# Hybrid decoder layer on one core: prompt attention without GpSimd, joined scores, longer decode waits

## The chip, the cores and the metric

One core of a Trainium2 chip runs the whole program. The metric is device microseconds from the start to the end of one execution; the median of several executions counts. The kernel before takes 2168.27 us (median of three, 2166.78 to 2168.47).

## The reference

One layer of a decoder runs for a prompt of 512 tokens and, with the same weights, for 8 sequences that each add one token to a cached window of 2048. All is in float32.

```
h = rmsnorm(x);  q, k, v, vc, gate_b, gate_c = split(h @ w_in)      # 2048 -> 6 x 1024
q, k = rmsnorm per head (16 heads of 64)
o = softmax over three dilated windows (128 step 1, 512 step 4, 2048 step 16) with a bias per distance
y = gate_b * conv3(gate_c * vc)
x += concat(rmsnorm(o), rmsnorm(y)) @ w_out
x += square(relu(rmsnorm(x) @ w_up)) @ w_down                       # 2048 -> 8192 -> 2048
```

The results are x, the new keys, values and convolution rows, and the cached windows moved on by one token.

## The kernel before

The 520 tokens (512 of the prompt, 8 of decode) are the columns of every matmul, in two halves of 260, and features lie on the partitions. A float32 operand is held as a rounded high part and the rest as a low part, and a product is three matmuls (high by high, high by low, low by high). ScalarE makes the high part by a copy into the rounded type, VectorE the low part by a subtract: lines 148 and 149 for the weights of the first stages, 419 and 420 for queries and keys, 482 and 483 for probabilities.

The program has a foreground and a background. The foreground is a row of projections. Each has 128 output features: two halves of the contraction, each of 8 blocks of 6 matmuls (`block`, line 213 holds the matmul). The first 24 projections are query, key and value for 8 pairs of heads; the next 24 are the three inputs of the convolution, 8 times; then come the output projection and the two layers of the MLP, which take the time after about 675 us.

The background is written as generators. `block` calls `step` twice per block, after its third and after its sixth matmul. A step moves on the first generator in `bgn` (norms of queries and keys) and then the first in `bg` (attention). A `yield` gives the turn back, and `wait(n)` yields n times, so a wait is a number of steps and thereby a place in the instruction order. All engines take their instructions in the order in which the program issues them: nothing is moved afterwards. After the fourth block of each half of a projection the weights of a later half are split (lines 148, 149). `drain` runs the steps that are left without any foreground between them; it is called after the 24 projections of the convolution (line 734).

After a query or key projection `ev_qkv` copies the result out of its bank with the norm's factor (line 529), squares it (lines 534 to 537, the squares again as a high and a low part), and puts `norm_gen` into `bgn`, to start 24 steps later, and not before the scores of the pair before are done. `norm_gen` sums the squares per head on TensorE (line 408, twice, once per half of the tokens), finishes the norm on ScalarE (411, 412) and VectorE (414 to 417), and writes the high and low parts of the normed rows (419, 420). After the value projection `attn_gen` is put into `bg`. It works on one pair of heads:

- transposes of the 8 decode rows and of the values (lines 433 to 444);
- for each of four query tiles of 128 rows: scores of both heads (`products`, line 456, into two banks from `stile`), bias, maximum and exponential (`score`, 463 to 466), division by the sum (`norm_p`, 472 and 473), and transposes of the first head's probabilities (`trans`, line 479 on TensorE into a bank from `wtile`, emptied by 482 and 483);
- the first head's product with the values (`pv`, line 489, emptied by 494 and 495);
- the second head's four transposes and its product.

The banks of PSUM: `mm` has two pairs for projections; `wtile` has two banks, which norms, transposes and the decode attention take in turn; `stile` has two, for scores and the products with the values. The third use of a name waits until the first has been read.

`dec_gen` follows the eighth pair in `bg` and runs beside the projections of the convolution: scores of the 8 decode tokens against gathered keys (VectorE, lines 603 and 609), softmax (629 to 636), transposes of the probabilities (641), then for each token three groups of gathered values: multiply (664), add (669), and a sum over the partitions on TensorE (674). At its end the sums are copied (680), transposed (684) and copied into the attention's result (687).

Of the kernel before, what the change touches and what calls it, by code (L numbers as in the profile page):

```python
# [25 lines left out]
F32 = mybir.dt.float32  # L26
# [11 lines left out]
E = 64  # L38
# [46 lines left out]
def hymba_kernel(ctx, tc, xT, wi, wo, wu, wd, state_k, state_v, sconv, relb, relrep, ohp, lcp, ohd, lcd,  # L85
# [118 lines left out]
    def wtile():  # L204
        return p2.tile([128, 512], F32, name="pw", bufs=2)
# [219 lines left out]
    def attn_gen(j):  # L425
        while done.get(("norm", j)) != 2:
            yield
        if j not in TB:
            load_T(j)
        yield from wait(1 if j else 10)  # L430
        st = wtile()
        for i in range(3):
            T.transpose(st[:NB, i * 128:(i + 1) * 128], flat(RAW[i, j])[:, SEQ:], ident)
        yield from wait(3)
        stg = wt((NB, 3, 128), name="stg")
        S.activation(stg.rearrange("p a b -> p (a b)"), st[:NB, :384], AF.Copy)
        SP.dma_start(scr_qkv[:, :, j * 128:(j + 1) * 128], stg)
        st = wtile()
        for s in range(4):
            T.transpose(st[:, s * 128:(s + 1) * 128], flat(RAW[2, j])[:, s * 128:(s + 1) * 128], ident)  # L440
        yield from wait(3)
        sv = st.rearrange("p (s h e) -> p h s e", s=4, h=2)
        S.activation(vv[:, :, :, 0], sv, AF.Copy)
        V.tensor_tensor(vv[:, :, :, 1], sv, vv[:, :, :, 0].bitcast(F32), OP.subtract)
        yield
        pt = {}

        def products(tb):

            w = (tb + 1) * 128  # L450
            q = slice(tb * 128, (tb + 1) * 128)
            ss = [stile() for _ in range(2)]
            for n, (a, b) in enumerate(((qh, kh), (qh, kl), (ql, kh))):
                for hp in range(2):
                    r = slice(hp * E, (hp + 1) * E)
                    T.matmul(ss[hp][:, :w], a[r, q], b[r, :w], start=n == 0, stop=n == 2)
            return ss

        def score(hp, tb, s):
            w = (tb + 1) * 128  # L460
            lg = late(j, tb) if hp else wt((128, 512), name="lg")
            sm = wk.tile([128, 4], F32, name="sm", bufs=8)
            V.tensor_tensor_reduce(out=lg[:, :w], in0=s[:, :w], in1=TB[j][:, hp, 512 - w:], scale=1.0, scalar=-3e38,
                                   op0=OP.add, op1=OP.max, accum_out=sm[:, 0:1])
            V.tensor_scalar(sm[:, 1:2], sm[:, 0:1], -1.0, None, op0=OP.mult)
            S.activation(lg[:, :w], lg[:, :w], AF.Exp, bias=sm[:, 1:2], accum_out=sm[:, 2:3])
            pt[hp, tb] = lg, sm

        def norm_p(hp, tb):
            w = (tb + 1) * 128  # L470
            lg, sm = pt[hp, tb]
            V.reciprocal(sm[:, 3:4], sm[:, 2:3])
            V.tensor_scalar(lg[:, :w], lg[:, :w], sm[:, 3:4], None, op0=OP.mult)

        def trans(hp, tb):
            lg, sm = pt.pop((hp, tb))
            st = wtile()
            for s in range(tb + 1):
                T.transpose(st[:, s * 128:(s + 1) * 128], lg[:, s * 128:(s + 1) * 128], ident)
            sv = st.rearrange("p (s t) -> p s t", s=4)[:, :tb + 1]  # L480
            q = slice(tb * 128, (tb + 1) * 128)
            S.activation(pth[:, :tb + 1, q], sv, AF.Copy)
            V.tensor_tensor(ptl[:, :tb + 1, q], sv, pth[:, :tb + 1, q].bitcast(F32), OP.subtract)

        def pv(hp):
            st = stile()
            for s in range(4):
                for n, b in enumerate((pth, ptl)):
                    T.matmul(st[:, s * 128:], vv[:, hp, s].rearrange("p c e -> p (c e)"), b[:, s, s * 128:],
                             start=s == 0 and n == 0, stop=s == 3 and n == 1, skip_group_check=True)  # L490
                yield
            r = slice(hp * E, (hp + 1) * E)
            o = flat(R3[:, j])[r, :SEQ]
            S.activation(o, st[:E, :], AF.Copy)
            V.tensor_tensor(o, st[E:, :], o, OP.add)
            yield

        for tb in range(4):
            ss = products(tb)
            for hp in range(2):  # L500
                score(hp, tb, ss[hp])
            yield from wait(4)
            if tb == 3:
                done["scores"] = j + 1
            for hp in range(2):
                norm_p(hp, tb)
            yield from wait(4)
            if tb:
                trans(0, tb - 1)
            yield from wait(3)  # L510
        if j < 6:
            toeplitz(j + 2)
        trans(0, 3)
        yield from wait(5)
        yield from pv(0)
        for tb in range(4):
            trans(1, tb)
            yield from wait(4)
        yield from wait(2)
        yield from pv(1)  # L520

    def ev_qkv(t, j, ps):
        raw = wt(name="raw")
        RAW[t, j] = raw
        if isinstance(ps, tuple):
            for h in range(2):
                V.tensor_tensor(raw[:, h], ps[h][:, :HT], rstd[:, h], OP.mult)
        else:
            V.tensor_tensor(raw, ps[:, :, :HT], rstd, OP.mult)
        if t == 1 and j:  # L530
            load_T(j)
        if t < 2:
            sh, sl_ = (wk.tile([128, 2, HT], F32R, name="sq", tag=g_, bufs=n_) for g_, n_ in (("w", 16), ("g", 4)))
            S.activation(sh, raw, AF.Square)
            sq = wt(name="tmp")
            P.tensor_tensor(sq, raw, raw, OP.mult)
            P.tensor_tensor(sl_, sq, sh.bitcast(F32), OP.subtract)
            hi, lo = (qh, ql) if t == 0 else (kh, kl)
            bgn.append([24 if j else 30, j, norm_gen(j, raw, (sh, sl_), qkgt[:, t:t + 1], hi, lo, okT[:, j] if t else None)])
        else:  # L540
            SP.dma_start(ovT[:, j], flat(raw)[:, :SEQ])
            bg.append(attn_gen(j))
# [18 lines left out]
    def dec_gen():  # L561
# [72 lines left out]
        yield from wait(2)  # L634
        V.reciprocal(sm[:, 3:4], sm[:, 2:3])
        V.tensor_scalar(lg, lg, sm[:, 3:4], None, op0=OP.mult)
        yield from wait(2)
        yield from wait(2)
        st = wtile()
        for g in range(3):  # L640
            T.transpose(st[:NP[g], g * 128:(g + 1) * 128], lg[:, GOFF[g]:GOFF[g] + NP[g]], ident)
# [17 lines left out]
        for n in range(len(items) + 1):  # L659
# [6 lines left out]
            if n and items[n - 1][1]:  # L666
# [2 lines left out]
                V.tensor_tensor(a[:NP[g]], a[:NP[g]], tiles.pop(("v", b, g))[:NP[g]], OP.add)  # L669
                if g == 2:  # L670
                    a = tiles.pop(("v", b, 0)).rearrange("p h e -> p (h e)")
                    yield from wait(10)
                    for c in range(4):
                        T.matmul(od[32 * c:32 * c + 32, :256], sel[:, 31 - b:63 - b], a[:, 256 * c:256 * c + 256],
                                 start=b == 0, stop=b == NB - 1, skip_group_check=True)
                    prev(n + 2)
# [584 lines left out]
```

## Time and profile before

| | us |
|---|---|
| three executions | 2166.78, 2168.27, 2168.47 |
| the profiled execution, its own time | 2167.66 |
| its span, first to last instruction | 2166.0 |
| TensorE matmuls busy | 2134.5 |
| VectorE, ScalarE, GpSimd busy | 1766.3, 957.9, 68.5 |

The profile shows one execution. A stage's limit is read from the engine that has no idle time in it, and the table of waits names for each idle time the instruction whose end let the engine go on. Times inside the trace count from the span's start. The projections of query, key and value run up to about 387 us, those of the convolution up to about 675 us.

### The profile page before, as it was taken

How to read it: one execution, taken by the hardware profiler on the slowest of the kernel's cores; microseconds unless marked ns; L12 is line 12 of the kernel's file. 1: busy time of each engine (PE TensorE's matmuls, PEld its weight loads, DVE VectorE, ACT ScalarE, POOL GpSimd, SP SyncE). 2: the span in 40 equal slices, each digit the busy share in tenths (PEclk: the TensorE clock that was granted, in tenths of full speed). 3: DMA queues.
4: the chain of work that ended last, by engine and by line, in shares of the span. 5: the costliest groups of instructions: out<-in, count | busy, mean ns of one | idle time of the engine just before them, and what ended most of it. 6: DMA issues, size and time to landing. Idle time of an engine off the chain costs nothing.

```text
span 2166.0 us, 42326 instructions
## 1 busy us (share of the span) xinstructions
PE 2134.5 (99%) x17594; PEld 2105.7 (97%) x17594; DVE 1766.3 (82%) x2421; ACT 957.9 (44%) x1379; POOL 68.5 (3%) x83
## 2 busy tenths in 40 slices
PE   8999999999999999999999999999999999999999
PEld 8888999999999999999999999999999999999999
DVE  7777776698786657798888888888999999999997
ACT  5444444321223235554444444445444444444443
POOL 1001010000000000000000000002000000000000
PEclk9999999999999999999999999999999999999999
DMA  5344543476464647666776676677876666666653
GB/s 208 124 165 148 169 161 113 139 229 210 153 186 155 245 155 243 226 221 241 253 236 219 245 246 215 246 253 269 314 291 250 225 226 251 231 224 246 239 200 122
DMA packets 137935, 459.83 MB, mean 212 GB/s; under 512 B 19504, under 2 KB 49840, under 8 KB 131344
## 3 DMA queue, kind: packets, MB, share of 16 engines
q1 hardware_dynamic: 136320, 454.81, 60.4%
q0 software_dynamic: 864, 2.10, 0.5%
q8 instruction: 138, 2.26, 0.4%
q14 instruction: 53, 0.43, 0.1%
q10 hardware_dynamic: 560, 0.22, 0.0%
HBM read 414.31 MB, written 181.16 MB: 275 GB/s over the span
## 4 chain that ended last, share of the span: by engine, by line
PE 63%; DVE 4%; ACT 1%; issue 1%; DMA 1%; DVEq 0%; SPq 0%
PE mn L1030 29%; PE mm L1030 29%; PE mm L213 5%; DVE R L788 1%; DVE wlo L149 1%; DVE wlo L788 1%; DVE x1t L934 0%; DVE acc L927 0%; DMA ra<-scr_a 0%; ACT sq L925 0%; ACT whi L148 0%; ACT x L936 0%; ACT R L936 0%; ACT R L787 0%; DMA ovs<-state_v 0%
## 5 line engine op out<-in xcount | busy, mean ns | idle before, releaser
L213 PE MATMUL mm<-R,whi 128*128 128x260 f32 x4000 | 677.7, 287 | 5.7 <-ACT whi L148 5.6
L213 PEld LDWEIGHTS mm<-R,whi 128*128 128x128 f32 x4000 | 560.8, 189 | 19.0 <-issue 8.6
L1030 PE MATMUL mm<-R,whi 128*128 128x260 f32 x3008 | 547.7, 283 | 1.7 <-ACT cs L1113 1.2
L1030 PE MATMUL mn<-R,whi 128*128 128x260 f32 x3008 | 547.5, 283 | 0.0
L1030 PEld LDWEIGHTS mm<-R,whi 128*128 128x128 f32 x3008 | 463.3, 188 | 2.1 <-ACT cs L1113 1.4
L1030 PEld LDWEIGHTS mn<-R,whi 128*128 128x128 f32 x3008 | 463.3, 188 | 0.1
L1030 PE MATMUL mn<-R,wlo 128*128 128x260 f32 x1504 | 425.0, 283 | 2.4 <-DVE wlo L788 2.4
L1030 PE MATMUL mm<-R,wlo 128*128 128x260 f32 x1504 | 425.1, 283 | 1.3 <-DVE wlo L788 1.3
L213 PE MATMUL mm<-R,wlo 128*128 128x260 f32 x2000 | 404.0, 284 | 0.0
L788 DVE TENSOR_TENSOR wlo<-raw,whi 128x1024 fp32r<-128x1024 f32 x255 | 311.9, 1223 | 109.3 <-ACT whi L787 107.5
L787 ACT ACTIVATE whi<-raw 128x1024 fp32r<-128x1024 f32 x255 | 269.3, 1056 | 207.4 <-PE mn L1030 95.3
L213 PEld LDWEIGHTS mm<-R,wlo 128*128 128x128 f32 x2000 | 310.0, 189 | 0.4
L787 ACT ACTIVATE whi<-rg 128x1024 fp32r<-128x1024 f32 x186 | 197.3, 1061 | 215.9 <-PE mn L1030 91.5
L1030 PEld LDWEIGHTS mn<-R,wlo 128*128 128x128 f32 x1504 | 283.2, 188 | 3.0 <-DVE wlo L788 3.0
L1030 PEld LDWEIGHTS mm<-R,wlo 128*128 128x128 f32 x1504 | 283.2, 188 | 1.8 <-DVE wlo L788 1.7
L788 DVE TENSOR_TENSOR wlo<-rg,whi 128x1024 fp32r<-128x1024 f32 x186 | 228.1, 1226 | 1.5 <-ACT whi L787 1.4
L148 ACT ACTIVATE whi<-raw 128x1024 fp32r<-128x1024 f32 (+1 forms) x129 | 133.7, 1038 | 167.5 <-PE mm L213 134.0
L149 DVE TENSOR_TENSOR wlo<-raw,whi 128x1024 fp32r<-128x1024 f32 (+1 forms) x129 | 155.5, 1206 | 45.6 <-ACT whi L148 43.6
L848 DVE TENSOR_TENSOR raw<-raw 128x1024 f32<-128x1024 f32 x62 | 75.6, 1219 | 0.0
L848 DVE TENSOR_TENSOR rg<-rg,raw 128x1024 f32<-128x1024 f32 x62 | 75.5, 1218 | 0.0
L848 DVE TENSOR_TENSOR raw<-rg,raw 128x1024 f32<-128x1024 f32 x60 | 73.5, 1225 | 2.1
L1150 DVE TENSOR_TENSOR yacc<-mm,yacc 128x520 f32<-128x520 f32 x96 | 66.6, 694 | 7.3 <-PE mm L1030 6.3
(227 smaller groups left out, 2291.2 us busy)
## 6 DMA issues: line engine op xcount, KB each, us to landing
oks<-state_k SPq DMA_DIRECT2D x184, 356.0 KB
ovs<-state_v SPq DMA_DIRECT2D x184, 356.0 KB
raw<-wi SPq DMA_DIRECT2D x94, 512.0 KB
raw<-wu SPq DMA_DIRECT2D x64, 512.0 KB
rg<-wd SPq DMA_DIRECT2D x64, 512.0 KB
raw<-wd SPq DMA_DIRECT2D x64, 512.0 KB
rg<-wu SPq DMA_DIRECT2D x60, 512.0 KB
raw<-wo SPq DMA_DIRECT2D x32, 512.0 KB
```

The lines of the kernel that those rows point to most:

```text
L148: S.activation(his[i][:, h], raws[i][:, h], AF.Copy)
L149: V.tensor_tensor(los[i][:, h], raws[i][:, h], his[i][:, h].bitcast(F32), OP.subtract)
L213: T.matmul(ps[t][:, :HT] if isinstance(ps, tuple) else ps[:, t, :HT], a[:, k, :], b[:, t, :], start=start and n == 0, stop=stop and n == 2)
L787: S.activation(hi, src, AF.Copy)
L788: eng.tensor_tensor(lo, src, hi.bitcast(F32), OP.subtract)
L848: e.tensor_tensor(o_, a_, b_, op)
L1030: T.matmul(ps[:, r, :HT], a[:, k, :], b(kt), start=n % 7 in ((0, 1, 3) if kts == 8 else (0, 1)) and kt == 0 and m == 0, stop=kt == kts - 1 ...
L1150: V.tensor_tensor(dst[:, r], v[:, r], dst[:, r], OP.add)
```

## The change

Four things change, all in the two attention generators and in `ev_qkv`.

- The squares of queries and keys: ScalarE squares, ScalarE copies that into the rounded type, and VectorE subtracts. GpSimd's multiply and subtract are gone.
- `products` takes a list of query tiles. Tiles 0 and 1 are computed in one go, side by side in the same two banks; tiles 2 and 3 stay single. The waits around them are now 5 steps, and the first head's transposes of tiles 0 and 1 follow the softmax of tile 2.
- The second head's transposes of tiles 0 and 2 take their bank from `stile`, those of tiles 1 and 3 from `wtile`.
- In `dec_gen` the wait ahead of the transposes of the probabilities is 10 steps instead of 4, and the wait ahead of each sum over the partitions is 14 instead of 10.

```diff
-        def products(tb):
+        def products(tbs):
             ss = [stile() for _ in range(2)]
-            for n, (a, b) in enumerate(((qh, kh), (qh, kl), (ql, kh))):
-                for hp in range(2):
-                    r = slice(hp * E, (hp + 1) * E)
-                    T.matmul(ss[hp][:, :w], a[r, q], b[r, :w], start=n == 0, stop=n == 2)
-            return ss
+            out, c = {}, 0
+            for tb in tbs:
+                w = (tb + 1) * 128
+                q = slice(tb * 128, (tb + 1) * 128)
+                for n, (a, b) in enumerate(((qh, kh), (qh, kl), (ql, kh))):
+                    for hp in range(2):
+                        r = slice(hp * E, (hp + 1) * E)
+                        T.matmul(ss[hp][:, c:c + w], a[r, q], b[r, :w], start=n == 0, stop=n == 2,
+                                 skip_group_check=True)
+                        out[hp, tb] = ss[hp][:, c:c + w]
+                c += w
+            return out
...
-        def trans(hp, tb):
+        def trans(hp, tb, st=None):
             lg, sm = pt.pop((hp, tb))
-            st = wtile()
+            st = st or wtile()
...
-        for tb in range(4):
-            ss = products(tb)
-            for hp in range(2):
-                score(hp, tb, ss[hp])
-            yield from wait(4)
-            if tb == 3:
+        ready = ()
+        for tbs in ((0, 1), (2,), (3,)):
+            both = [(hp, tb) for tb in tbs for hp in range(2)]
+            ss = products(tbs)
+            for b in both:
+                score(*b, ss[b])
+            yield from wait(5)
+            if tbs == (3,):
                 done["scores"] = j + 1
-            for hp in range(2):
-                norm_p(hp, tb)
-            yield from wait(4)
-            if tb:
-                trans(0, tb - 1)
-            yield from wait(3)
+            for b in both:
+                norm_p(*b)
+            yield from wait(5)
+            for tb in ready:
+                trans(0, tb)
+                yield from wait(3)
+            ready = tbs
+            yield from wait(1)
...
         for tb in range(4):
-            trans(1, tb)
+            trans(1, tb, None if tb % 2 else stile())
             yield from wait(4)
...
-            S.activation(sh, raw, AF.Square)
             sq = wt(name="tmp")
-            P.tensor_tensor(sq, raw, raw, OP.mult)
-            P.tensor_tensor(sl_, sq, sh.bitcast(F32), OP.subtract)
+            S.activation(sq, raw, AF.Square)
+            S.activation(sh, sq, AF.Copy)
+            V.tensor_tensor(sl_, sq, sh.bitcast(F32), OP.subtract)
...
-        yield from wait(2)
-        yield from wait(2)
+        yield from wait(10)
         st = wtile()
...
-                    yield from wait(10)
+                    yield from wait(14)
                     for c in range(4):
```

## Rows read from the trace of the kernel before

**Rows 1.** The page's first part: busy time, share of the span, instructions.

```profile
PE 2134.5 (99%) x17594; PEld 2105.7 (97%) x17594; DVE 1766.3 (82%) x2421; ACT 957.9 (44%) x1379; POOL 68.5 (3%) x83
```

**Rows 2.** TensorE's waits: waiting line, releaser, total us, times, longest.

```profile
PE pw L479 <- DVE R L483: 9.1, 11, 1.3
...
PE pw L408 <- DVE h L414: 1.5, 3, 0.9
...
PE pw L641 <- DVE lg L636: 0.9, 1, 0.9
```

**Rows 3.** Busy time by window (us; instructions), granted clock, DMA share, GB/s.

```profile
48.00:424.00 376.00, 363.80 (x2924) 345.25 (x2923) 264.15 (x633) 172.97 (x366) 33.95 (x33) 1.00 0.44 147
...
680.00:860.00 180.00, 180.00 (x1496) 179.82 (x1495) 118.87 (x184) 70.41 (x111) 1.91 (x2) 1.00 0.59 205
```

**Rows 4.** The same view, around 133 us.

```profile
131.00:132.50 1.50, 0.35 (x2) 0.14 (x2) 1.47 (x5) 0.00 (x0) 0.00 (x0) 1.00 0.12 52
...
133.20:135.60 2.40, 2.40 (x13) 2.40 (x13) 1.58 (x4) 1.39 (x3) 0.00 (x0) 0.50 0.00 0
```

**Rows 5.** Timeline, GpSimd and VectorE near 128 us, VectorE at 266: start, us, instruction.

```profile
127.66 1.06 POOL L536 TENSOR_TENSOR tmp<-raw 128x520 f32<-128x520 f32 x1 [13.15 <-DVE sm L472]
...
127.69 1.31 DVE L473 TENSOR_SCALAR lg<-lg,sm 128x512 f32<-128x512 f32 x1
...
265.96 0.49 DVE L473 TENSOR_SCALAR lg<-lg,sm 128x512 f32<-128x512 f32 x1
```

**Rows 6.** Groups by line, 48 to 424 us: count, busy us, mean ns, idle before.

```profile
L420 DVE TENSOR_TENSOR R<-raw,R 128x520 fp32r<-128x520 f32 x16 | 11.2, 697 | 6.6 <-ACT R L419 6.6
...
L534 ACT ACTIVATE sq<-raw 128x520 fp32r<-128x520 f32 x14 | 8.9, 639 | 24.5 <-DVE raw L529 24.5
```

**Rows 7.** Timeline of a steady pair, 269 to 282 us.

```profile
269.94 0.48 DVE L415 SCALAR_TENSOR_TENSOR raw<-raw,qkgt,h 128x260 f32<-128x260 f32 x1
...
271.69 0.70 DVE L529 TENSOR_TENSOR raw<-mm,rstd 128x520 f32<-128x520 f32 x1 [0.46 <-PE mm L213]
...
273.60 1.31 POOL L537 TENSOR_TENSOR sq<-tmp,sq 128x520 fp32r<-128x520 f32 x1
...
273.97 0.43 DVE L414 SCALAR_TENSOR_TENSOR h<-pw,h 128x260 f32<-128x260 f32 x1 [1.58 <-ACT h L412]
274.32 0.88 DVE L415 SCALAR_TENSOR_TENSOR raw<-raw,qkgt,h 128x260 f32<-128x260 f32 x1
...
277.10 0.55 PE L479 MATMUL pw<-ident,R 128*128 128x128 f32 x3 [0.69 <-DVE R L483]
...
277.92 1.23 DVE L149 TENSOR_TENSOR wlo<-raw,whi 128x1024 fp32r<-128x1024 f32 x1
...
280.18 0.69 DVE L483 TENSOR_TENSOR R<-pw,R 128x512 fp32r<-128x512 f32 x1 [0.56 <-ACT R L482]
...
281.50 0.63 PE L489 MATMUL pS<-R 128*128 128x512 f32 x2
```

**Rows 8.** Timeline, scores of query tiles 0 and 1 of one pair.

```profile
109.77 0.55 PE L456 MATMUL pS<-R 64*128 64x128 f32 x6
...
114.39 0.62 PE L456 MATMUL pS<-R 64*128 64x256 f32 x6
```

**Rows 9.** Timeline, end of the convolution's projections.

```profile
664.99 1.21 DVE L669 TENSOR_TENSOR kv<-kv 96x1024 f32<-96x1024 f32 x1
...
666.26 0.64 PE L674 MATMUL pw<-kv,sel 128*32 128x256 f32 x8 [1.01 <-DVE kv L669]
666.97 0.38 ACT L680 ACTIVATE os<-pw 128x256 f32<-128x256 f32 x1 [4.83 <-PE pw L674]
...
669.46 0.38 PE L684 MATMUL pw<-ident,os 128*128 128x128 f32 x2
...
674.91 0.70 DVE L719 TENSOR_TENSOR c<-mm,rstd 128x520 f32<-128x520 f32 x1 [2.55 <-PE mm L213]
...
677.83 0.69 DVE L728 TENSOR_TENSOR acc_c<-acc_c,sq 128x520 f32<-128x520 f32 x1
```

More of the change, by code (lines that the diff above doesn't have):

```diff
@@ L446, in attn_gen @@
         pt = {}
-        def products(tb):
-            w = (tb + 1) * 128
-            q = slice(tb * 128, (tb + 1) * 128)
+        def products(tbs):
             ss = [stile() for _ in range(2)]
-            for n, (a, b) in enumerate(((qh, kh), (qh, kl), (ql, kh))):
-                for hp in range(2):
-                    r = slice(hp * E, (hp + 1) * E)
-                    T.matmul(ss[hp][:, :w], a[r, q], b[r, :w], start=n == 0, stop=n == 2)
-            return ss
+            out, c = {}, 0
[10 more added lines that the diff above has]
+            return out
         def score(hp, tb, s):
```

## The prediction

> **What bounds the kernel now.** I read the page first: TensorE is busy in 99% of the span, VectorE in 82%, GpSimd in 3% [rows 1]. So time is won or lost only where TensorE waits. The table of TensorE's waits says for whom: 9.1 us at line 479, the transposes of the probabilities, until VectorE has emptied an earlier transpose bank (line 483), 1.5 us at line 408, and 0.9 us in the decode attention at line 641 [rows 2]. The windows say where: between 48 and 424 us TensorE is busy for 363.8 of 376 us and VectorE for 264, 70%; after 680 us TensorE has no gap [rows 3]. What moves the end of the two attention stages therefore moves the end of the kernel by as much. A wait also costs clock: after an idle stretch that ended at 132.5 us, in which TensorE was busy for 0.35 of 1.5 us, the granted clock was 0.50, which is 1.2 GHz [rows 4]. At half speed these 2.4 us lose 1.2, and with the flanks of the stretch I take 1.7 us for one such drop.
>
> **The unit of the sum.** In the gapless stretch 1496 matmuls take 180 us, 0.120 us each [rows 3]. The kernel calls its background generators once per three projection matmuls, so a step is 0.36 us. A projection has 32 steps, a pair of heads 96. The issue order of both kernels can be counted in steps by hand from the waits in the code.
>
> **Part 1, GpSimd's two operations become a square and a copy on ScalarE and a subtract on VectorE (16 times, two per pair).** It removes GpSimd's 1.1 and 1.3 us [rows 5, 7]; no TensorE wait names them. It returns time to VectorE: beside GpSimd line 473 took 1.31 us, by itself 0.49 [rows 5], and line 415 took 0.88 and 0.48 [rows 7]. In the steady pairs (the fourth to seventh) one of each is stretched, about 1.1 us a pair; in the first three two of line 473, 1.7 us. Over eight pairs that is about 10 us. It adds on VectorE 16 subtracts, each like line 420 (0.70 us [rows 6]), 11 us, and a wait: the subtract stands in VectorE's queue right behind line 529, which makes its input, and needs a square and then a copy of 0.64 us each on ScalarE [rows 6]. VectorE stands still for 1.4 us, 22 us over the stage. That wait is the new thing: everything behind it on VectorE is late by 2.1 us, less what was returned.
>
> Who waits for that? In a steady pair take the end of the key projection as zero, 271.4 us in the trace (line 529 follows at 271.69 [rows 7]). Now: line 414 at 274.0, the last line 483 from 280.18 to 280.87, and the second head's products with the values (line 489) at 281.50, after one wait of 0.7 to 0.9 us at the transposes at 277.10 [rows 7]. With the change VectorE's queue is, in order: line 495 (now two steps earlier, ahead of 529) to 1.15; 529 to 1.8; wait for square and copy to 3.2; subtract to 3.9; the first small 483 to 4.1; 414 to 417 to 5.8, with their ScalarE part done by 4.2; 420 behind its ScalarE copy to 7.2; the second 483 to 7.6; line 149, 1.2 us [rows 7], to 9.0; the last two 483 (0.55 and 0.69) to 10.1. TensorE reaches the products 19 steps after zero, 6.9 us, plus 0.8 us for the ten transposes on the way (three in a row last 0.55 [rows 7], so one more costs TensorE less than 0.11) and some 0.2 us around them: 7.9. So it waits **2.2 us** there. Where line 483 can start earlier than I chain it, the wait falls to nothing; where ScalarE is late as well it grows to 3. I take 2.2, since nearly every link has its duration in a row.
>
> **Part 2, half of the second head's transposes use the score banks.** The wait at 277.10 goes: the bank that those transposes now take was freed by line 495. That is -0.9 us in each of four steady pairs. But what is late next is the product above, so the four pairs together go by 4 x (2.2 - 0.9) = **+5.2**. In the first three pairs the order differs, since the first starts late; of the 10.6 us at lines 479 and 408 [rows 2] some 7 to 8 lie there, and the clock's 1.7. Walking the new order there in the same way I find 2.7 us at lines 408 and 479 and 2.0 at 489 in the first, 3.7 in all in the second (line 408 wants a bank that the new square and copy release late), 0.9 in the third: 9.3 against about 9.3. I take **0** for the three, with 5 either way; the eighth pair has no norms beside it and stays.
>
> **Part 3, the scores of the first two query tiles in one go.** Alone, six matmuls of 128 columns delay the projection matmuls by about 0.57 us, those of 256 columns by 0.64 (their rows last 0.55 and 0.62 [rows 8]), and the first projection matmul after each is followed 0.1 us late. I take 0.11 us for each of three further pairs inside a run, so the joined run costs some 0.97: 0.35 us won per pair, **-2.8** in all; between none and 0.57 x 8 = 4.6. The DMA of the bias tile moves two steps earlier on SP's queue, ahead of nothing that TensorE waits for.
>
> **Part 4, the decode attention waits longer.** Its order now: last add (line 669) 664.99, product 666.26 after 1.0 us of wait, copy 666.97, transposes 669.46 [rows 9]; the last projection matmul is issued at 674.6, 0.3 us ahead of line 719 [rows 9], 14 steps behind the transposes and 12 behind the copies that follow two steps later. The change adds 6 steps ahead of line 641 (its 0.9 us wait goes, taken as **-1**), 4 steps at each of 8 products, and takes 2 off the last prompt pair: 36. So the decode chain ends 24 steps behind the projections. The code then runs the rest at once, with no projection matmul between. Counted back from the end, the last add is 23 steps away, so add, product, copy and transposes all fall there. TensorE's queue holds the product ahead of the output projection. VectorE: lines 719 to 728 end at 678.5 as now [rows 9]; the add takes 1.2 us to 679.7. TensorE stands from 674.7: **5.0 us**. Then 0.7 to the copy, 0.4 for it and 0.2 to the transposes: 6.3 less the 0.8 us of work and the 1.0 us of wait that are there now: **+4.5**. A longer idle stretch than that of [rows 4] should cost the same clock drop: **+1.7**. If VectorE's add got in front of the convolution's work, it would be 2 us less. The kernel's two small output DMAs wait on ScalarE's queue behind the copies; nothing needs them. Value loads come up to four steps later, and stay two items ahead.
>
> **Sum**: +5.2 + 0 - 2.8 - 1 + 4.5 + 1.7 = +7.6 on the profiled execution's 2167.66, which is 0.6 below the median of 2168.27: **2175.3 us**. A measurement of this kernel can tell about 0.2% (4.3 us) from no change.
>
> **Rivals.**
> *The freed port wins (faster).* If VectorE catches up, the products with the values never wait, and the old waits (10.6 and 1.7) go with the 2.8 of part 3 and 1 of line 641; at the end the decode tail takes 6.2. That gives 2167.7 - 16.1 + 6.2 = 2158; with half of the old waits left, 2164. For it: the waits near 131 us lie right behind line 473 stretched to 1.31 [rows 5]. It decides where VectorE's new standing still falls into the 30% in which it idles anyway [rows 3]. Against: VectorE gets about 10 us and pays 33. A rule speaks for more. The Trainium skill (SBUF — State Buffer, "SBUF: two separate sides") says that VectorE and GpSimd share a port pair under an exclusive lock held for a whole instruction, the loser blocked; by it all of GpSimd's 33.9 us of the stage could come back, as much as is paid, and this rival's 2158 would be the forecast. The trace agrees for lines 473 and 415, but where 414 ran as GpSimd did, it kept its 0.43 us [rows 7], so I stay with the 10 us. Chance 0.17.
> *The new wait only replaces the old (same).* If the products wait 0.9 instead of 2.2, the four pairs give 0: 2170. For it: the chain has ten handovers, each of which I may have too slow, and TensorE's own lateness shortens the next wait. Chance 0.25; within it, that the tail of part 4 stays hidden, 2169.
> *Slower than forecast.* Each 2.2 us wait could bring a clock drop; four of them at 1.7 give 2182. The trace shows a drop after the idle stretch of [rows 4] and none after the wait at 277.10. This lies inside my forecast's chance.
>
> **How the numbers follow.** Forecast (part 1's wait and part 4's tail both there): 0.58, 2172 to 2183. Same: 0.25. Faster: 0.17. Cut at 0.2%, the first gives slower 0.58, and of the third 0.01 falls to the second: same 0.26, faster 0.16. The range takes in the same case and the mild end of the faster one: 2163 to 2183.
>
> **What would show it.** Right: TensorE waiting at line 489 for line 483 about 2 us in each of four pairs; none at 479 there; an idle stretch of about 5 us where the convolution's projections end, and the clock at half behind it; no GpSimd beside line 473. Wrong: the decode's transposes still ahead of the last projection, or line 489 never waiting, which would say that VectorE's order has slack that I did not see.

## The result, and the profile after

The changed kernel takes 2184.18 us (median of four, 2182.19 to 2184.97); the kernel before took 2167.88 in the same comparison. The ratio is 1.0076 with a 95% interval of 1.0064 to 1.0089: 16.3 us more. The sum of the prediction had 7.6 us more. The sign was right, and the time lies 1.2 us beyond the upper end of the range.

In the code after, lines from 456 on have moved: 473 is now 478, 479 is 484, 482 and 483 are 487 and 488, 489 is 494, 494 and 495 are 499 and 500, 529 is 538, the new square, copy and subtract are 544 to 546, 674 is 682, 680 is 688, 684 is 692, 719 and 728 are 727 and 736. Lines up to 420 have kept their numbers.

The page's first part, after [rows 1]:

```profile
PE 2139.8 (98%) x17594; PEld 2111.7 (97%) x17594; DVE 1762.7 (81%) x2437; ACT 968.7 (44%) x1395; POOL 27.8 (1%) x51
```

The table of waits, after [rows 2]: waiting line, releaser, total us, times, longest.

```profile
PE pw L408 <- DVE h L414: 7.4, 2, 4.2
...
PE pw L682 <- DVE kv L677: 4.8, 1, 4.8
...
PE pS L494 <- DVE R L488: 4.6, 5, 1.0
...
PE pS L494 <- ACT R L487: 2.2, 4, 0.6
...
PE pw L484 <- DVE R L488: 0.4, 1, 0.4
...
DVE sq L546 <- ACT sq L545: 22.0, 16, 1.4
```

The 9.1 us at the transposes (line 479 before, 484 now) are down to 0.4, and the wait at the old line 641 is gone. In their place stand 7.4 us at the norm's sums, 6.8 at the products with the values (4.6 for VectorE, 2.2 for ScalarE) and 4.8 in the decode attention. VectorE's new standing ahead of the subtract is 22.0 us in 16 times, 1.4 us each, the figure that the prediction chained from two ScalarE operations.

The windows, after [rows 3, 4]: us, then busy time and instructions of TensorE, its weight loads, VectorE, ScalarE and GpSimd, granted clock, DMA share, GB/s.

```profile
48.00:424.00 376.00, 358.08 (x2850) 341.35 (x2849) 254.53 (x641) 179.23 (x377) 0.78 (x5) 0.98 0.42 141
...
680.00:860.00 180.00, 174.67 (x1433) 173.34 (x1432) 112.23 (x172) 67.84 (x106) 1.92 (x2) 0.98 0.55 193
...
91.20:94.50 3.30, 3.30 (x17) 3.30 (x16) 2.12 (x5) 1.39 (x3) 0.00 (x0) 0.50 0.03 11
...
135.50:142.20 6.70, 6.04 (x28) 6.04 (x29) 4.37 (x12) 2.86 (x6) 0.00 (x0) 0.50 0.13 51
...
333.50:336.80 3.30, 3.30 (x16) 3.30 (x16) 0.00 (x0) 0.43 (x1) 0.00 (x0) 0.50 0.00 0
381.30:384.60 3.30, 3.30 (x17) 3.30 (x15) 0.00 (x0) 0.09 (x1) 0.00 (x0) 0.50 0.00 0
...
685.10:691.80 6.70, 4.87 (x26) 3.99 (x27) 1.30 (x3) 1.73 (x4) 0.00 (x0) 0.50 0.06 13
```

Read the instruction counts first. From 48 to 424 us TensorE got through 74 matmuls fewer than before, from 680 to 860 us 63 fewer; at 0.120 us each [rows 3] that is 8.9 and 7.6 us. Between the two windows it got through 14 more (2135 for 2121), since the end of the decode attention has moved beyond 680; that takes 1.7 us off, and 14.8 of the 16.3 us are found. Then the clock. Two windows of the kernel before had 1.00 [rows 3] and have 0.98 now, because in five places TensorE ran at 1.2 GHz: 20.8 us of busy time in all (3.30 + 6.04 + 3.30 + 3.30 + 4.87). Half of that, **10.4 us**, is lost. The kernel before had one such place. [rows 4] show 2.4 us of it; all of it is 3.30 us, of which half, 1.65 us, is lost:

```profile
132.60:135.90 3.30, 3.30 (x16) 3.30 (x17) 2.48 (x5) 1.39 (x3) 0.00 (x0) 0.50 0.00 0
```

These counts are those of one profiled execution. The mean clock of the changed kernel's four executions goes from 0.993 to 0.995, so the low places need not be the same in each.

The timeline of a steady pair, after [rows 7]: start, us, instruction, in brackets the idle time before it. The key projection ends at 275.9.

```profile
276.36 0.69 DVE L500 TENSOR_TENSOR R<-pS,R 64x512 f32<-64x512 f32 x1 [0.86 <-ACT R L499]
277.08 0.70 DVE L538 TENSOR_TENSOR raw<-mm,rstd 128x520 f32<-128x520 f32 x1
...
279.16 0.70 DVE L546 TENSOR_TENSOR sq<-tmp,sq 128x520 fp32r<-128x520 f32 x1 [1.38 <-ACT sq L545]
...
281.34 0.43 DVE L417 SCALAR_TENSOR_TENSOR raw<-h,raw 128x260 f32<-128x260 f32 x1
...
282.48 0.70 DVE L420 TENSOR_TENSOR R<-raw,R 128x520 fp32r<-128x520 f32 x1 [0.71 <-ACT R L419]
...
283.70 1.22 DVE L149 TENSOR_TENSOR wlo<-raw,whi 128x1024 fp32r<-128x1024 f32 x1 [0.18 <-ACT whi L148]
284.59 0.49 PE L494 MATMUL pS<-R 128*128 128x512 f32 x1 [0.57 <-ACT R L487]
...
285.31 0.68 DVE L488 TENSOR_TENSOR R<-pw,R 128x512 fp32r<-128x512 f32 x1
...
286.04 0.50 PE L494 MATMUL pS<-R 128*128 128x512 f32 x1 [0.96 <-DVE R L488]
```

Counted from 275.9, the ends of VectorE's seven lines are 1.15, 1.9, 4.0, 5.9, 7.3, 9.0 and 10.1; the prediction had 1.15, 1.8, 3.9, 5.8, 7.2, 9.0 and 10.1. TensorE stands twice, ahead of the first matmul of the product and of the second. The last projection matmuls before it, three, start at 283.49 and are issued by 283.85 (0.12 us each); the first of the product starts 0.74 us later, and the second 1.45 us after that, where two that don't wait follow each other in 0.13 (a row of this is shown further down). That is 0.74 + 1.32 = 2.1 us against the forecast of 2.2, and TensorE arrived 7.95 us after the key projection, for 7.9.

The end of the convolution's projections, after [rows 9]:

```profile
685.16 1.22 DVE L677 TENSOR_TENSOR kv<-kv 96x1024 f32<-96x1024 f32 x1
686.43 1.08 PE L682 MATMUL pw<-kv,sel 128*32 128x256 f32 x8 [4.82 <-DVE kv L677]
687.58 0.38 ACT L688 ACTIVATE os<-pw 128x256 f32<-128x256 f32 x1 [3.21 <-PE pw L682]
688.01 0.69 PE L692 MATMUL pw<-ident,os 128*128 128x128 f32 x2 [0.50 <-ACT os L688]
```

TensorE stands for 4.82 us (forecast 5.0) behind VectorE's convolution work and its last add. The same product that took 0.64 us before [rows 9] takes 1.08, and the clock of the 6.7 us that contain it is 0.50.

### The profile page after: what moved, and what is told of

It is laid out like the page before. It is cut to its first block, busy times and chain, and to the rows that moved or that the text cites. A ratio compares the mean times of both kernels' runs of the same rounds, so it can differ in the third digit from the quotient of the medians.

```text
span 2181.9 us, 42282 instructions
## 1 busy us (share of the span) xinstructions
PE 2139.8 (98%) x17594; PEld 2111.7 (97%) x17594; DVE 1762.7 (81%) x2437; ACT 968.7 (44%) x1395; POOL 27.8 (1%) x51
## 4 chain that ended last, share of the span: by engine, by line
PE 83%; DVE 9%; ACT 4%; DMA 3%; issue 1%; SPq 0%; DVEq 0%; ACTq 0%
PE mn L1038 29%; PE mm L1038 28%; PE mm L213 22%; DVE wlo L149 2%; DMA raw<-wi 1%; ACT whi L148 1%; PE pS L494 1%; PE pS L458 1%; DMA ra<-scr_a 1%; DVE R L796 1%; DVE wlo L796 1%; DVE sc L618 1%; PE pw L484 0%; DVE kv L612 0%; DVE x1t L942 0%
```

## The experiments

The waits were foreseen nearly to the tenth, yet the loss is twice the forecast. Two questions follow. **What do the parts cost one by one**, and is the wait at the products really the squares' work, as the prediction has it? The theory at this point: the square and copy hold up VectorE's queue, and the waits cost further time by the clock; the rival: the new order of the steps alone brings TensorE to the products too early. All times below are medians with the kernel before measured beside them; the interval of each ratio reaches some 2 to 4 us to either side, so a smaller difference between two kernels rests on its trace. Nothing of the computation is left out in any of these kernels; three of them add matmuls whose results are not used.

### Part 4 undone, alone, and kept busy

First the changed kernel with the decode waits of before:

```diff
-        yield from wait(10)
+        yield from wait(2)
+        yield from wait(2)
...
-                    yield from wait(14)
+                    yield from wait(10)
```

> The changed kernel with the decode waits of before (4 steps ahead of the transposes of the probabilities, 10 ahead of each sum). Theory: the decode chain ends ahead of the last projection again, so the 5.1 us of idle TensorE at the end of the convolution's projections, the 1.1 us behind it and the 6.8 us at half clock go, and the two old waits of about 1 us come back: 7 us less than the changed kernel's 2184.2, about 2177. Rival (the tail is hidden, all the loss is in the prompt attention): 2184, within 2 us.

Measured: 2177.46 against 2166.87, ratio 1.0049 (1.0034 to 1.0064): 10.6 us of the 16.3 are left, so part 4 costs 5.7. The reverse edit in the kernel before:

> The kernel before, with only the longer waits of the decode attention (10 steps and 14 steps). By the count of steps 26 are left at the end of the convolution's projections. Theory: an idle stretch of about 5 us there and half clock behind it, the two old waits gone: 6 to 7 us slower, 2174. Rival (the tail costs only where the attention ahead of it has changed): 2168.

2173.49 against 2167.35, ratio 1.0029 (1.0018 to 1.0041): 6.1 us. Its table of waits shows the standing (line 673 here is 674 of before), and line 479 as before [rows 2]:

```profile
PE pw L479 <- DVE R L483: 9.1, 11, 1.3
...
PE pw L673 <- DVE kv L668: 4.8, 1, 4.8
```

How much of that is the clock? In the changed kernel 36 matmuls of 260 columns, into a bank of `stile` that nothing reads, were put ahead of the last product:

```diff
+                    if b == NB - 1:
+                        dum = stile()
+                        for _ in range(36):
+                            T.matmul(dum[:, :HT], R0[:, 0, 0, 0, :128], R0[:, 0, 0, 0, :], start=True, stop=True)
```

> The changed kernel, with 36 projection-sized matmuls into a free score bank issued just ahead of the last sum over the partitions, so that TensorE works through most of its 5.1 us of idle time there; their results are not used. Theory (the idle stretch costs time twice, as a wait and by the clock after it): the 6.8 us at half clock behind the stretch go, 3 us less, 2181. Rival (the clock costs nothing here): 2184 or more.

2181.10 against 2167.12, ratio 1.0060 (1.0045 to 1.0075): 14.0 us in place of 16.3. The timeline and the window of that place:

```profile
681.26 4.44 PE L684 MATMUL pS<-R 128*128 128x260 f32 x36
...
686.25 0.64 PE L686 MATMUL pw<-kv,sel 128*32 128x256 f32 x8 [0.55 <-DVE kv L677]
```

```profile
685.10:691.80 6.70, 5.64 (x51) 4.95 (x50) 2.33 (x2) 1.73 (x4) 0.00 (x0) 1.00 0.05 11
```

The wait is as long as before, only filled with work, and the product is back at 0.64 us and the clock at 1.00. So the 4.82 us of standing do bring the low clock, and it costs here 2.4 us by half of the 4.87 us of busy time, on top of the standing itself; the medians say 2.3, which by themselves would be within the noise.

### Part 1 alone, and GpSimd back

In the kernel before only the squares were changed:

```diff
-            S.activation(sh, raw, AF.Square)
...
-            P.tensor_tensor(sq, raw, raw, OP.mult)
-            P.tensor_tensor(sl_, sq, sh.bitcast(F32), OP.subtract)
+            S.activation(sq, raw, AF.Square)
+            S.activation(sh, sq, AF.Copy)
+            V.tensor_tensor(sl_, sq, sh.bitcast(F32), OP.subtract)
```

> The kernel before, with only the squares of queries and keys moved from GpSimd to ScalarE and VectorE. Theory: VectorE's new wait makes the transposes at line 479 wait longer in the steady pairs than the 0.9 us of before: 4 to 12 us slower, 2172 to 2180. Rival (the end of GpSimd's hold on VectorE is worth more): 2168 or less.

2175.19 against 2166.87, ratio 1.0039 (1.0024 to 1.0054): 8.3 us slower. So the time that VectorE gets back from GpSimd does not pay for the new standing. The first of its rows of waits stands against 9.1 in 11 times [rows 2], the second is new:

```profile
PE pw L479 <- DVE R L483: 12.6, 15, 1.5
...
PE pw L479 <- DVE h L414: 1.4, 4, 0.3
```

With lines 408 and 433 these waits are 17.9 us, 11.5 before: 6.4 of the 8.3. The clock has no part in it, its mean in the profiled execution is 1.000.

The reverse edit, GpSimd's two operations put back into the changed kernel:

> The changed kernel with the squares of queries and keys as before: one square on ScalarE, multiply and subtract on GpSimd. Theory (VectorE's wait behind line 529 makes the loss): TensorE's wait at the second head's products falls from 2.1 us to under 0.7 in the fourth to seventh pair, the waits of 3.4 and 4.3 us at the norms' matmul in the first two pairs fall to 1.5 or less, and the attention's low-clock stretches (17 us) mostly go: about 2166. Rival (the joined scores and the score banks make the new waits): no stretch of these goes, 2180 or more.

2175.38 against 2166.87, ratio 1.0039 (1.0024 to 1.0054). It gave back 7.8 us, as much as the part costs alone, but 8.5 us are still lost, where full repair of the attention stage was expected. The product's wait is not gone:

```profile
PE pw L408 <- DVE h L414: 5.9, 2, 3.5
...
PE pS L494 <- DVE R L488: 4.7, 5, 1.0
...
PE pS L494 <- ACT R L487: 1.2, 4, 0.7
```

Its larger part, ahead of the second matmul, is as long as in the changed kernel; the smaller one shrinks, and the clock is 1.00 in all four steady pairs. The timeline of one of them:

```profile
234.91 0.49 PE L494 MATMUL pS<-R 128*128 128x512 f32 x1 [0.16 <-ACT R L487]
236.37 0.50 PE L494 MATMUL pS<-R 128*128 128x512 f32 x1 [0.96 <-DVE R L488]
```

So the theory falls in one point: the wait stands mostly on the new order of the steps, and the squares lengthen it by some 0.5 us. The rows say by how much that order brings TensorE forward: before, it issued the products 10.1 us after the key projection, of which some 0.8 was waiting at the transposes [rows 7]; now it reaches them after 7.95, 1.3 us earlier.

### Which queue passes the delay on

If it is VectorE's standing of 1.4 us, then the subtract can be issued nine steps later, when its input has long been there:

```diff
-            V.tensor_tensor(sl_, sq, sh.bitcast(F32), OP.subtract)
+            later.append([8, partial(V.tensor_tensor, sl_, sq, sh.bitcast(F32), OP.subtract)])
```

(`step` counts the entries of `later` down and calls each when it is due.)

> The changed kernel, with the subtract of the squares issued 9 steps later than the copy it waits for, so that VectorE finds its input ready. The same work on every engine. Theory (the wait is the cause): nearly the same gain as with GpSimd back, 2165 to 2172, and VectorE's idle time ahead of the subtract gone. Rival (the added work on ScalarE and VectorE is the cause): over 2179.

2185.72 against 2166.87, ratio 1.0085 (1.0068 to 1.0102): no gain. The timeline of VectorE in a steady pair (line 493 is 488 of the changed kernel):

```profile
281.98 0.29 DVE L493 TENSOR_TENSOR R<-pS,R 128x128 fp32r<-128x128 f32 x1 [1.54 <-ACT R L492]
...
287.50 0.69 DVE L188 TENSOR_TENSOR sq<-tmp,sq 128x520 fp32r<-128x520 f32 x1
...
288.58 0.68 DVE L493 TENSOR_TENSOR R<-pw,R 128x512 fp32r<-128x512 f32 x1
```

VectorE no longer waits for the copy of the squares, but stands for 1.54 us for the high parts of a transpose instead: ScalarE has the square and the copy, 1.3 us, in its own queue ahead of them. And the subtract, moved, now lies ahead of the last subtracts that the product wants: the idle time ahead of the product's second matmul is 1.57 us here, 0.96 in the changed kernel. The test of this reading moves ScalarE's copy as well, together with the subtract and by 19 steps, for the keys alone:

```diff
-            S.activation(sh, sq, AF.Copy)
-            V.tensor_tensor(sl_, sq, sh.bitcast(F32), OP.subtract)
+            def rest():
+                S.activation(sh, sq, AF.Copy)
+                V.tensor_tensor(sl_, sq, sh.bitcast(F32), OP.subtract)
+
+            later.append([18 if t else -1, rest])
+            if not t:
+                later.pop()[1]()
```

> The changed kernel, with the keys' rounding copy on ScalarE and the subtract behind it issued 19 steps later, after the second head's transposes; the queries' stay. Theory (ScalarE's queue is the link: its added copy stands ahead of the norm's logarithm and exponential, on which VectorE's line 414 waits): the wait at the products falls from 2.1 us to about 1.3 as with GpSimd back, 2176 to 2180. Rival (the added VectorE work is the cause, wherever it stands): over 2183.

2174.88 against 2167.12, ratio 1.0032 (1.0019 to 1.0044): 7.8 us slower than before instead of 16.3. VectorE's and TensorE's timeline (line 493 is 488 of the changed kernel, 499 is 494):

```profile
276.23 0.29 DVE L493 TENSOR_TENSOR R<-pS,R 128x128 fp32r<-128x128 f32 x1 [0.87 <-ACT R L492]
...
281.49 0.50 PE L499 MATMUL pS<-R 128*128 128x512 f32 x1
...
282.95 0.50 PE L499 MATMUL pS<-R 128*128 128x512 f32 x1 [0.96 <-DVE R L493]
```

VectorE's stand for the high parts is 0.87 us instead of 1.54, shorter by the copy. The first of the product's two waits is gone, the second is as long as ever: about the picture with GpSimd back, but without GpSimd. So the squares cost their part through the places of three instructions in two queues, ScalarE's copy among them, and not through VectorE's standing alone. The copy and the subtract were moved together here, and the subtract further than in the run before, so their shares are not told apart.

### Parts 2 and 3 in the order of before

Only the banks of the second head's transposes changed, in the kernel before:

```diff
-            st = wtile()
+            st = st or wtile()
...
-            trans(1, tb)
+            trans(1, tb, None if tb % 2 else stile())
```

> The kernel before, with only the second head's transposes of tiles 0 and 2 in the score banks. Theory: the wait of 0.9 us at line 479 in the steady pairs goes, TensorE reaches the second head's products 0.9 us earlier and still finds them ready or waits under 0.4 us there, since they stay two steps later than in the changed kernel: 2162 to 2165. Rival (the banks bring the wait at the products with them): a wait of over 1 us at line 489 in each steady pair, 2168 or more.

2163.65 against 2167.12, ratio 0.9982 (0.9973 to 0.9991): 3.5 us faster, a small gain, but its interval leaves no room for none. Line 479's waits for line 483, 9.1 us before, are 3.5, and the steady pairs wait for line 495 instead, at most 0.4 us:

```profile
PE pw L479 <- DVE R L483: 3.5, 3, 1.2
...
PE pS L479 <- DVE R L495: 1.5, 4, 0.4
```

With the joined scores of tiles 0 and 1 put where tile 0's scores were, and every other step where it was before:

```diff
+        ss = products((0, 1))
+        for b in ((0, 0), (1, 0), (0, 1), (1, 1)):
+            score(*b, ss[b])
+        yield from wait(7)
+        for b in ((0, 0), (1, 0), (0, 1), (1, 1)):
+            norm_p(*b)
+        yield from wait(12)
+        trans(0, 0)
+        yield from wait(3)
+        for tb in (2, 3):
...
```

> The kernel before, with the second head's transposes in the score banks and the scores of tiles 0 and 1 joined at tile 0's place, every later step where it was before; squares on GpSimd, decode waits of before. Theory: the joined scores alone give 2.8 us on the 2163.7 of the banks alone: 2161. Rival (the joined run delays the softmax and gives it back): 2164 or more.

2161.12 against 2167.85, ratio 0.9970 (0.9958 to 0.9982): 6.7 us faster, so the joined scores are worth some 3.2 beside the banks. Taken alone, parts 1 to 4 then sum to +8.3 - 3.5 - 3.2 + 6.1 = +7.7, and the change measured +16.3. That 7.7 lies beside the forecast's 7.6 is luck: the forecast was made for the new order, and these parts were run in the old one. The other 8.6 us are left for the rest of part 3, the waits of 5 steps and the regrouped transposes, which set the new order, and for what the parts do to each other. That order was not run by itself; GpSimd back without part 4 gives it by subtraction, if parts add up: 8.5 - 6.1 = +2.4 against -6.7 in the old order, 9.1 us.

### What the clock adds in the attention stage

In the changed kernel, 14 unused matmuls stand ahead of the second head's product of the steady pairs, in that product's own bank:

```diff
+            if hp and 3 <= j <= 6:
+                for _ in range(14):
+                    T.matmul(st[:, :HT], R0[:, 0, 0, 0, :128], R0[:, 0, 0, 0, :], start=True, stop=True)
```

> The changed kernel, with 14 projection-sized matmuls into the product's own bank ahead of the second head's products in the fourth to seventh pair, 1.7 us of the 2.1 us that TensorE waits there; they are overwritten. Theory (clock and wait are two costs): the two low-clock stretches behind those products go and the products start when they did, 3 us less, 2181. Rival (the clock costs nothing of its own, or the extra matmuls delay the products): 2184 or more.

2179.63 against 2167.35, ratio 1.0060 (1.0045 to 1.0075): 12.3 us in place of 16.3. The windows behind the two waits that had dropped the clock:

```profile
333.50:336.80 3.30, 3.30 (x29) 3.30 (x28) 0.69 (x1) 1.62 (x3) 0.00 (x0) 1.00 0.02 5
...
381.30:384.60 3.30, 3.30 (x30) 3.30 (x29) 1.71 (x2) 2.44 (x4) 0.00 (x0) 1.00 0.02 5
```

29 and 30 matmuls run in 3.3 us instead of 16 and 17. The two drops were worth 3.3 us by the windows and some 4 by the times. The same was done for the two long waits at line 408 of the first two pairs, with 26 and 36 matmuls:

```diff
+            if t and k_out is None and j in (1, 2):
+                for dum, n_ in ((stile(), j * 5 + 8), (stile(), j * 5 + 8)):
+                    for _ in range(n_):
+                        T.matmul(dum[:, :HT], R0[:, 0, 0, 0, :128], R0[:, 0, 0, 0, :], start=True, stop=True)
```

> The changed kernel, with 26 and 36 projection-sized matmuls into the score banks in the two long waits (3.4 and 4.3 us) at the norms' matmul; their results are not used. Theory: the 3.4 and 6.8 us at half clock behind these waits go, 4 to 5 us less, 2179 to 2180. Rival: 2184 or more.

2183.09 against 2167.35, ratio 1.0075 (1.0060 to 1.0090): a miss, 15.7 us in place of 16.3, no gain that can be told from none. The windows say why:

```profile
91.20:94.50 3.30, 3.25 (x26) 3.16 (x27) 1.79 (x4) 1.39 (x3) 0.00 (x0) 1.00 0.04 17
...
238.10:241.40 3.30, 3.30 (x16) 3.30 (x15) 0.09 (x1) 0.69 (x2) 0.00 (x0) 0.51 0.00 0
285.80:289.10 3.30, 3.30 (x17) 3.30 (x16) 0.00 (x0) 0.39 (x1) 0.00 (x0) 0.50 0.00 0
```

The low clock at 91 and at 135 us went, as meant; but behind the steady waits at 238 and 286 us, where the changed kernel had kept the full clock, it came, so that now all four steady pairs drop.

### Repairs

If TensorE only comes too early to the second head's product, six more steps ahead of it are enough:

```diff
-        yield from wait(2)
+        yield from wait(8)
         yield from pv(1)
```

> The changed kernel, with 8 instead of 2 steps of wait ahead of the second head's products, so that TensorE has 6 more steps (2.2 us) of projection matmuls there. Theory (VectorE's chain is late by about 2.1 us and nothing else waits): the wait at the products goes in all pairs, the two clock drops behind it too; the decode tail is 6 steps longer and costs the same: 8 to 12 us less, 2172 to 2176. Rival (the loss moves on to the next wait): 2181 or more.

2169.17 against 2167.12, ratio 1.0009 (0.9999 to 1.0018): 14 us better than the changed kernel, more than expected. The products now run without a wait, both matmuls in one row of the timeline, and the clock of all four steady pairs is 1.00. The low clock is not gone from the kernel: it stands behind waits of the first and the third pair, near 90 and 182 us, and at the tail.

```profile
284.89 0.62 PE L494 MATMUL pS<-R 128*128 128x512 f32 x2
```

With part 4 undone as well:

> The changed kernel with 8 steps ahead of the second head's products and the decode waits of before. Theory (the two losses add): 15 us from the first, 7 from the second, so 2162, 5 below the kernel before; left over are the first pairs' waits at the norms' matmul. Rival (they overlap): 2166 or more.

2163.34 against 2167.85, ratio 0.9977 (0.9967 to 0.9987): the two losses add. With GpSimd back too:

> As the run before it, but the squares on GpSimd again. Theory: with the products moved later, VectorE's and ScalarE's lateness has no TensorE wait left in the steady pairs, so the squares' place matters in the first pairs alone: within 4 us of that run, 2158 to 2162. Rival (the squares cost 8 us wherever the products stand): 2154.

2159.07 against 2167.85, ratio 0.9958 (0.9942 to 0.9975). And with the keys' copy and subtract 19 steps later in place of GpSimd:

> The changed kernel with the keys' copy and subtract later, 8 steps ahead of the second head's products, and the decode waits of before. Theory: the steady pairs have no wait left to lose, so against the run without the later copy only the first two pairs gain: 2157 to 2161. Rival: no difference, 2162.

2159.16 against 2167.85, ratio 0.9960 (0.9946 to 0.9975). Both beat the kernel before by about 9 us and the changed one by 25. They can't be told apart: GpSimd can be dropped at no price, if the copy does not stand where it delays others.

## Why the prediction was right or wrong

**Right: the chain and the waits.** Each of its seven places was met to 0.1 us, the wait at the products is 2.1 for 2.2, that at the decode tail 4.82 for 5.0, line 641's wait is gone, and the transposes hardly wait. The joined scores gave 3.2 for 2.8, part 4 cost 5.7 to 6.1 for 5.2 (+4.5 + 1.7 - 1). VectorE's standing of 22 us was exact. One reading goes beyond its rows: they show TensorE without a gap from 680 to 860 us, but from 860 to 2160 us it is busy for 1292.87 of 1300. This did no harm, since it is 1292.62 in the changed kernel.

**Wrong: the clock.** The step that failed is the count of drops: the sum holds "+1.7" for one further drop, at the tail, and takes back as much for the old one, "the clock's 1.7", within its 0 for the first three pairs. Net it puts the clock at nothing. The runs showed five places at half clock and 10.4 us lost, against 1.65 before: 8.8 more, where the time missed the sum by 8.7. Two of the places lie behind the steady waits, which the sum takes as plain waits, "4 x (2.2 - 0.9)"; the prediction named them in its rival "Slower than forecast" and left them out, since the wait at 277.10 had brought none [rows 7]; but that row shows 0.69 us, and a wait three times as long was judged by it. Two lie behind the stands at line 408 in the first two pairs, which the walk had found (2.7 and 3.7 us) and given no price of the clock, though the stretch of 1.5 us of [rows 4] had one. The size of one drop, 1.7, was right for the kernel before and the steady pairs (1.65 from 3.30) and too small behind the longer stands: 3.0 at 135 us and 2.4 at the tail.

**The first three pairs.** The prediction found 9.3 us of waits there, and the trace has 9.2, but not all in the places it gave: in the first pair 3.22 and 0.44 at lines 408 and 484 (for 2.7) and 0.80 at 494 (for 2.0), in the second 4.18 (for 3.7), in the third 0.59 (for 0.9). That the sum agrees so well is in part luck. Up to 200 us the table of waits has, beside the 7.4 of line 408 and the 0.4 of line 484 shown above:

```profile
PE pS L494 <- DVE R L488: 0.8, 1, 0.8
...
PE pS L484 <- DVE R L500: 0.6, 1, 0.6
```

The waits that went were 8.0 us up to 200 (6.1 at line 479, 1.5 at 408, 0.4 at 489), so the term is +1.2 without the clock. The longest but one, in the timeline:

```profile
86.25 1.22 DVE L149 TENSOR_TENSOR wlo<-raw,whi 128x1024 fp32r<-128x1024 f32 x1 [1.83 <-ACT whi L148]
...
88.58 0.42 DVE L414 SCALAR_TENSOR_TENSOR h<-pw,h 128x260 f32<-128x260 f32 x1
89.05 0.51 PE L408 MATMUL pw<-sq,bd 128*128 128x260 f32 x2 [3.22 <-DVE h L414]
```

Line 414 comes late here in part because VectorE has first waited 1.83 us for the high part of a weight. With GpSimd back the two waits at line 408 are still 5.9 of the 7.4 us, so they too stand mostly on something else than the squares.

With what was measured in their place, the prediction's own terms are 4 x (2.1 - 0.9) + 1.2 - 3.2 - 0.9 + 4.5 + 8.8 = +15.2, for 16.3 measured. Waits that no term has are 0.7 us at the scores of the first pair (line 458) and 0.9 more than before at the transposes of the decode rows (line 433, 1.8 for 0.9).

**Right in time, wrong in cause.** The prediction put the steady wait into part 1, as the work of the square, copy and subtract. Its step "TensorE reaches the products 19 steps after zero" used the new order, and that order is the larger cause: with GpSimd back 1.3 to 1.6 us of the wait stay. And its link, "everything behind it on VectorE is late by 2.1 us, less what was returned", was one of two: with VectorE's standing removed by itself the time did not fall, since ScalarE's queue carried the same delay and the moved subtract stood in a new place ahead of the product.

**The rivals.** "The freed port wins" is refuted by the squares alone, +8.3 us. What it rests on is real: from 48 to 424 us line 473 (478 now, 64 times in both) took 34.6 us before and takes 24.8, line 415 17.3 and 15.4; that is 11.7 us back, for about 10 in the prediction. The Trainium skill (SBUF — State Buffer, "SBUF: two separate sides") states that a VectorE instruction in a 2-port mode or with two inputs in SBUF and a GpSimd instruction that reads SBUF take a shared port pair under an exclusive lock, and the later one blocks; the trace agrees in that these two lines take less time now. Line 414, which the prediction held against that rule, reads one of its two inputs from PSUM (`pw`), so its 0.43 us do not speak against it. But VectorE's time was not what TensorE waited for. "The new wait only replaces the old" fell with the 2.1 us. "Slower than forecast", at 2182, came nearest, though of its four drops two came, and the others elsewhere.

## What to carry to other kernels

Where a queue runs in issue order, the price of an operation is its place: the same square, copy and subtract cost 8.3 us where they were put, and nothing that could be measured with the copy issued 19 steps later and the product that they delayed 6 steps later. Before two edits are priced apart, ask whether one of them also moves the consumer forward: here the regrouped steps cost about 9 us, by subtraction, and hid two parts that win 6.7. A wait of TensorE that is foreseen should be priced twice, for the standing and for the clock behind it, and the second price taken from a stand of the same length.

## What was not expected of the hardware

The low clock behind a wait is not a matter of that wait's length alone. The same 2.1 us at the products (idle times of 0.57 and 0.96 us ahead of two matmuls) were followed by half clock in two of the four steady pairs of the changed kernel, in one of four with part 4 undone, and in four of four with the earlier waits filled; with the subtract alone moved, where the idle times are longer (0.56 and 1.57 us), in one of four; behind the waits of 1.3 to 1.6 us of the two kernels with GpSimd back or the copy late, it came in none of eight. Each of these counts is of one execution, and executions of one kernel differ: of thirteen of the kernel before, measured together, three had a mean clock of 1.000 and took 2166.4 to 2166.7 us, ten had 0.998 or 0.999 and took 2167.3 to 2168.8. So a count of drops is a sample, and what decides between waits of equal length stays open. And a drop's cost could be had back without shortening the wait: unused matmuls in the stand kept the clock at 1.00, for 2.4 us at the tail and 3.3 in the two steady pairs by the windows.
